# Down projection of a SwiGLU layer: a ninth weight tile in seven products, and two held plain tiles instead of three

## The chip, the cores and the metric

The kernel runs on one core of one Trainium2 chip. The metric is the device time of one execution in microseconds (us). A core has a matmul engine (TensorE, PE in the profile), a vector engine (VectorE, DVE), a scalar engine (ScalarE, ACT), a general engine (GpSimd, POOL) and a queue engine (SyncE, SP) that issues most of the transfers. Each engine works through its own instructions in order; semaphores make one wait for another.

## The reference

One decoder block on 256 tokens of width 1024, in float32: two token mixers side by side, an output projection, a layer norm, a SwiGLU feed-forward layer, and a second layer norm. The change lies in the last step, the down projection of the feed-forward layer.

```python
D_MODEL = 1024
SEQ = 256
D_FF = ((8 * D_MODEL + 3 * 256 - 1) // (3 * 256)) * 256   # 2816
...
    mixed = jnp.einsum('bsc,cd->bsd', g_a * z_a + g_b * z_b, w_out)
    x = layer_norm(DN_ALPHA * x + mixed, ln1_w, ln1_b)

    h = jnp.einsum('bsd,df->bsf', x, w_ffn_in)
    h_gate, h_up = jnp.split(h, 2, axis=-1)
    y = jnp.einsum('bsf,fd->bsd', jax.nn.silu(h_gate) * h_up, w_ffn_down)
    return layer_norm(DN_ALPHA * x + y, ln2_w, ln2_b)
```

## The kernel before

**Weights.** All weights are cut into 77 tiles of 128 x 2048 numbers (`plan`), each loaded once into one of three `raw` buffers by SP. A float32 product is made from three faster ones: ACT casts the tile to a short form (`wh`), DVE subtracts that from the original (`wl`), and PE adds up `wh` times the high part of the activations, `wl` times the high part, and `wh` times the low part. `stage` and `stage_fast` do this for the next tile of the list, and `fetch` calls them so that three items stand ready ahead of the one handed out. There are four `wh` and four `wl` buffers. In the last stage the order of PE, DVE and ACT is the order of the program; the other queues are ordered by the compiler's scheduler, which also hands out the buffers of each pool, among them 12 slots of 128 x 2048 (`big`, through `slot`).

**The down projection.** It has 11 tiles, each for 256 rows of `w_ffn_down` (a pair of 128) and all 1024 columns. A tile times its activations is a product of 2 x 2 blocks: two halves of the tokens by two blocks of rows by two halves of the columns, eight block products of 512 columns, three matmuls each, so 24 matmuls. A *fast* tile (`fast`, from line 1050) does it with seven block products of sums of blocks, 21 matmuls, as in Strassen's scheme. It needs seven blocks of activation sums (made in `ffn_step`, lines 1026 to 1031: four operations of DVE and one split) and seven blocks of weights: three of the four quarters of the tile as they are (`corners`) and four sums of quarters (`sums`). The item `corners` is used by 9 matmuls, then `sums` by 12.

The string `DOWN` gives the order: `S` is a fast tile whose weight sums DVE makes in SBUF (three additions, `make_sums`), `T` a fast tile whose sums are made by transfers in DRAM and then loaded, `P` a plain tile. Before, it is `STTSTTSTPPP`: eight fast tiles (the column pairs `FAST`, 2 to 9), then three plain ones (`PLAIN`, the pairs 0, 1 and 10). `sum_weights` makes one T tile's sums: two copies on SP's queue and four accumulating transfers on POOL's, each of the last two after what it reads. It is called behind the loads of the tiles in `SUMS_AFTER`. `BESIDE` lists the raw items that are loaded into a slot of `big` instead of a `raw` buffer.

Token half 0 and half 1 share the banks `p1`, `p5`, `p6` and `p7` in the fast tiles; `into_residual` (line 1061) adds these to the residual on DVE after the last fast tile.

**The held tiles.** The last `HOLD_DOWN` tiles are plain and held. In the loop they are multiplied for token half 0 alone (12 matmuls each), so that half 0's layer norm can run while PE does half 1. For half 1 PE then does `p3` with the first held tile, two opening matmuls (lines 1139 and 1140), `p3` with the other held tiles, the edge (258 columns, line 1145) and `more` (256 columns, line 1146), 6 matmuls a tile each. The edge's columns hold the sums of the weights' rows too, so the mean of half 1 is known before `more` is done: line 1167 takes it, 1168 to 1171 are the squares on ACT, 1177 and 1178 the variance and its root, 1181 the output. ACT's copies into the edge and `more` banks (lines 1141 to 1143) come behind the opening matmuls and ahead of half 0's squares (line 1154). The squares of half 0 are needed by line 1158.

**The activations' pairs.** Pairs 0 and 1 are computed early (`FfnEarly`). Pair 10 comes out of the last `ffn_step`; before, it is a plain tile's, its product is handed back as `last_gate` and split after the first fast tile (line 1081). The activation sums of each fast pair live in a slot, but for the first (spare tiles) and the last (the unused half of a plain slot, and the tile `masks`).

Of the kernel before, what the change touches and what calls it, by code (L numbers as in the profile page):

```python
# [10 lines left out]
F32 = mybir.dt.float32  # L11
F32R = mybir.dt.float32r
U32 = mybir.dt.uint32
# [4 lines left out]
P = 128  # L18
# [6 lines left out]
NF = FF // P  # L25
LEVELS = 7
# [10 lines left out]
BLOCKS = 32  # L37
GROUPS = ((0, 1), (2, 3), (4, 5, 6))
HQ_WIDE = 4
HOLD_DOWN = 3  # L40
SUMS = 2
ORDERED = 2
LAGS = (0,1,3,5)
DOWN = "STTSTTSTPPP"
SUMS_AFTER = (36, 41, 50, 54, 58)
FAST = tuple(range(2, 2 + len(DOWN) - DOWN.count("P")))
PLAIN = tuple(q for q in range(NF // 2) if q not in FAST)
SEQUENCE = [PLAIN[DOWN[:i].count("P")] if s == "P" else FAST[i - DOWN[:i].count("P")] for i, s in enumerate(DOWN)]
BESIDE = ((3, "corners"), (4, "sums"), (6, "corners"), (7, "corners"), (7, "sums"))
SUMMED = [q for q, s in zip(SEQUENCE, DOWN) if s == "T"]  # L50

C_ID = 0
# [3 lines left out]
C_MASK = C_CAUSAL + 3 * P  # L56
C_END = C_MASK + LEVELS * P
# [27 lines left out]
def plan():  # L85

    tiles = []

    def add(w, k0, kn, c0, n, held=False):
        tiles.append((w, k0, kn, c0 if isinstance(c0, tuple) else (c0,), n, held))  # L90

    def feat(w, c0, n):
        for c in range(c0, c0 + n, 256):
            add(w, 0, 8, c, 256)

    def tok(w, c0, n):
        for c in range(c0, c0 + n, 512):
            add(w, 0, 4, c, 512)
            add(w, 4, 4, c, 512)

    feat("w_in", 0, 1024)
    tok("w_in", 2048, 1024)
    tok("w_in", 3072, 1024)
    tok("w_in", 6144, 512)
    tok("w_in", 8192, 1024)
    for c in range(2):
        if c == 1:
            tok("w_in", 6144 + 512, 512)
        for j in range(2 * c, 2 * c + 2):
            feat("w_in", 5120 + j * 256, 256)  # L110
            feat("w_in", 4096 + j * 256, 256)
    tok("w_in", 7168, 1024)
    tok("w_branch_a", 0, 1024)
    tok("w_branch_b", 0, 1024)
    for k in range(0, KC, 2):
        add("w_out", k, 2, 0, 1024)
    for j in range(0, EARLY, 2):
        for k in range(0, KC, 4):
            add("w_ffn_in", k, 4, (j * P, FF + j * P), 256, j < HOLD_IN)
    for j in range(EARLY, NF, 2):  # L120
        add("w_ffn_in", 0, 8, j * P, 256)
        add("w_ffn_in", 0, 8, FF + j * P, 256)
    for q in SEQUENCE:
        add("w_ffn_down", 2 * q, 2, 0, 1024)
    return tiles
# [3 lines left out]
def hybrid_layer_kernel(ctx: ExitStack, tc, x, xw, vecs, bias, wts, ln1_w, ln1_b, ln2_w, ln2_b, consts, out):  # L129
    nc = tc.nc  # L130
    pool = lambda name, bufs, **kw: ctx.enter_context(tc.tile_pool(name=name, bufs=bufs, **kw))
    cp = pool("cp", 1)
# [12 lines left out]
    def r32(ap):  # L145
        return ap.bitcast(F32)
# [31 lines left out]
    tiles = plan()  # L178
# [4 lines left out]
    ready = []  # L183
    held_down = range(len(tiles) - HOLD_DOWN, len(tiles))
    last_raw = []
    corners = {}
# [4 lines left out]
    def split(dst_h, dst_l, src):  # L191
        nc.scalar.copy(dst_h, src)
        nc.vector.tensor_sub(dst_l, src, r32(dst_h))
# [5 lines left out]
    def stage(pieces=None, eng=nc.vector):  # L199
# [18 lines left out]
        for ks in ks_of(pieces or (k,)):  # L218
            nc.sync.dma_start(raw[:, ks, :], src[:, ks, :])
            if i in SUMS_AFTER and ks.start == 0:  # L220
                sum_weights(down[SUMMED[SUMS_AFTER.index(i)]])
            nc.scalar.copy(h[:, ks, :], raw[:, ks, :])  # L222
# [7 lines left out]
    def sum_weights(i):  # L230


        b, s = quarters(wts[i]), quarters(summed[i])
        tc.keep_in_program_order(nc.sync.dma_start(s[:, 0:2, :], b[:, 1:3, :]))
        tc.keep_in_program_order(nc.sync.dma_start(s[:, 2:4, :], b[:, 2:4, :]))
        more = lambda dst, src: nc.gpsimd.dma_start(dst, src, accum_op=ALU.add)  # L236
        for n in range(2):
            more(s[:, n, :], b[:, 0, :])
        more(s[:, 2, :], s[:, 0, :])
        more(s[:, 3, :], s[:, 2, :])  # L240

    def stage_fast(i, kind):


        def make_sums(b):
# [7 lines left out]
        at = SEQUENCE.index(next(q for q in FAST if down[q] == i))  # L253
        raw = lambda: quarters(slot(f"raw{kind}{i}") if (at, kind) in BESIDE else
                               wraw.tile([P, 2048], F32, tag="raw", name=f"raw{kind}{i}"))
# [47 lines left out]
    xp = Pair("xp")  # L303
    xTh, xTl = Pair.Part(xp, 0), Pair.Part(xp, 1)
    vec = cp.tile([P, 3 * H], F32, tag="vec", name="vec")
    cst = cp.tile([P, C_MASK], F32, tag="cst", name="cst")
    msk = cp.tile([P, C_END - C_MASK], F32, tag="masks", name="masks")
    ident = cst[:, C_ID:C_ID + P]
    causal = cst[:, C_CAUSAL:C_MASK]
    cos = cst[:, C_COS:C_COS + T]  # L310
    sin = cst[:, C_SIN:C_SIN + T]
    masks = msk.bitcast(U32).rearrange("p (l t) -> p l t", l=LEVELS)
    ones = cp.tile([P, P], F32R, tag="ones", name="ones")
    half = cp.tile([P, 4], F32, tag="half", name="half")

# [110 lines left out]
    with tc.manual_schedule(engines={ET.PE, ET.DVE, ET.Activation}):  # L426
# [40 lines left out]
        add(range(4, 8))  # L467
        for f in range(4, 8):
            forget(f)
    for z, a, b in ((cst, 0, C_MASK), (msk, C_MASK, C_END)):  # L470
        tc.keep_in_program_order(nc.sync.dma_start(z, consts[:, a:b]))
    for j in range(4):
        sg = sm.tile([P, 2, T], F32, tag="sg", name=f"sgq{j}")
        sgs = [by_half(sg[:, f, :]) for f in range(2)]
        if j < HQ_WIDE:
            for f, ps in enumerate(wide_pair(f"hq{j}", xp, mm, "mm")):
                z = Qg[:, :, 2 * j + f, :]
# [413 lines left out]
    def row_parts(name, widths, n0=0):  # L891
        parts = []
        for i, (p, w) in enumerate(widths):
# [9 lines left out]
    apl = [slot(f"ap{i}", F32R).rearrange("p (q u k t) -> p q u k t", q=2, u=2, k=2)  # L903
           for i in range((len(PLAIN) + 1) // 2)]
    act_plain = {q: apl[i // 2][:, i % 2] for i, q in enumerate(PLAIN)}

    def fast_parts(i):
        if i == 0:
            tiles = [klp.tile([P, H * P], F32R, tag="kl", name="ash"), cp.tile([P, D], F32R, tag="bgr", name="asl")]
        elif i == len(FAST) - 1:  # L910
            tiles = [apl[-1][:, 1].rearrange("p u k t -> p (u k t)"), cp.tile([P, 7 * P], F32R, tag="masks", name="asl7")]
        else:
            both = slot(f"as{i}", F32R)
            tiles = [both[:, 0:1024], both[:, 1024:2048]]
        return [z[:, 0:7 * P].rearrange("p (b t) -> p b t", b=7) for z in tiles]
# [46 lines left out]
    with tc.manual_schedule(engines={ET.PE, ET.DVE, ET.Activation}):  # L962
# [3 lines left out]
        tiles = [(2 * q,) + fetch(0) for q in range(4)]  # L966
# [42 lines left out]
    room = slot("room").rearrange("p (n b t) -> p n b t", n=2, b=8)  # L1009
    def ffn_step(j):  # L1010
        q = j // 2
        z = room[:, q % 2]
        gate, up = [z[:, b:b + 4, :].rearrange("p (f t) c -> p f (t c)", f=2) for b in (0, 4)]
        for nm, p, tag, s in [("g", mm, "mm", gate), ("u", aux, "aux", up)]:
            for f, ps in enumerate(wide_pair(f"f{nm}{j}", x1p, p, tag)):
                nc.scalar.copy(s[:, f, :], ps[:, 1, :])
                nc.vector.tensor_add(s[:, f, :], ps[:, 0, :], s[:, f, :])
            if nm == "g":
                nc.scalar.activation(s, s, AF.Silu)
        nc.vector.tensor_mul(gate, gate, up)  # L1020
        if q in PLAIN:
            if q < NF // 2 - 1:
                split(act_plain[q][:, 0], act_plain[q][:, 1], gate)
            return gate

        nc.vector.tensor_sub(z[:, 4, :], z[:, 0, :], z[:, 2, :])
        nc.vector.tensor_sub(z[:, 5, :], z[:, 4, :], z[:, 1, :])
        nc.vector.tensor_sub(z[:, 6, :], z[:, 1, :], z[:, 0, :])
        nc.vector.tensor_add(z[:, 7, :], z[:, 3, :], z[:, 5, :])
        act_fast[q] = fast_parts(FAST.index(q))  # L1030
        split(*act_fast[q], z[:, 1:8, :])
# [3 lines left out]

    with tc.manual_schedule(engines={ET.PE, ET.DVE, ET.Activation}):
        for j in range(NF - 2 * ORDERED, NF, 2):
            last_gate = ffn_step(j)
        bank = lambda p, n: p.tile([P, 512], F32, tag="aux" if p is aux else "mm", name=n)
        p2, p4, p1, p5 = [bank(mm, f"wp{i}") for i in (2, 4, 1, 5)]  # L1040
        p7, p3, wd0, p6 = [bank(aux, f"wp{i}") for i in (7, 3, 0, 6)]
# [35 lines left out]
        for i, q in enumerate(SEQUENCE):  # L1077
            if q in FAST:
                fast(q)
                if q == FAST[0]:  # L1080
                    split(act_plain[PLAIN[-1]][:, 0], act_plain[PLAIN[-1]][:, 1], last_gate)
                if q == FAST[-1]:
                    wb2 = bcast("wb2", ln2_w, ln2_b)
                    into_residual()
                continue
            tile_q = [(2 * q,) + fetch()]
            if i < len(SEQUENCE) - HOLD_DOWN:
                for part in late:
                    rows_pass([part], lhs, 1, tile_q, first=2 * begins[id(part[0])], **ends)
            else:  # L1090
                held += tile_q
            for part in early:
                rows_pass([part], lhs, 0, tile_q, first=2 * begins[id(part[0])], **ends)
        y = slot("y").rearrange("p (t d) -> p t d", t=NT)
        z, spare = [slot("z")[:, i:i + D] for i in (0, D)]
# [3 lines left out]

        ends_h, ends_l = [slot(f"e{n}", F32R)[:, 0:HOLD_DOWN * 2 * 264].rearrange("p (i k c) -> p i k c", i=HOLD_DOWN, k=2)  # L1100
                          for n in "hl"]
        edges = []
        sums = sm.tile([P, 2 * HOLD_DOWN], F32, tag="bst", name="wsum")
        for i, (raw, (k0, wh, wl)) in enumerate(zip(last_raw, held)):
# [112 lines left out]
```

## Time and profile before

| | |
|---|---|
| median of 3 runs | 485.95 us (485.85 to 488.02) |
| the profiled execution | 485.77 us |
| its span, first to last instruction | 484.0 us |
| PE busy | 476.5 us, 2956 matmuls |
| DVE busy | 387.8 us |
| ACT busy | 294.1 us |
| POOL busy | 58.2 us |
| DMA | 108.70 MB, mean 225 GB/s |
| the fast tiles | 422.57 to 460.77 us |
| the held tiles | 460.77 to 477.73 us |
| the rest, without PE | 477.73 to 484.0 us |

The profile is of one execution. Its span begins with the first instruction and ends with the last; the device time is 1.8 us more. Matmuls overlap, so PE's busy time tells that it had work, not how fast it was; the distance between the starts of two matmuls tells that.

### The profile page before, as it was taken

To read this page: it belongs to the slowest core of one execution; us is meant where nothing else is said; L and a number is where in the kernel's file an instruction comes from. 1 tells how busy PE (TensorE), PEld (TensorE's weight loads), DVE (VectorE), ACT (ScalarE), POOL (GpSimd) and SP (SyncE) were. 2 spreads that over 40 slices of the span, in tenths; PEclk is the share of its full clock that TensorE was granted. 3 is DMA by queue.
4 is the path that set the end of the run, shared out by engine and by line. 5 is a ranking of instruction groups with operands and counts; after the bars stand their busy time and mean duration, and the time that the engine had idled before them with its cause. 6 is when DMAs were issued, how large, how long until landed. Compare 5 with 4: busy or idle time off the path is not lost.

```text
span 484.0 us, 7438 instructions
## 1 busy us (share of the span) xinstructions
PE 476.5 (98%) x2956; PEld 409.0 (85%) x2956; DVE 387.8 (80%) x504; ACT 294.1 (61%) x408; POOL 58.2 (12%) x62
## 2 busy tenths in 40 slices
PE   9999999999999999999999999999999999999994
PEld 8888888788899888888888888888888888888884
DVE  4889895799957889999566778853887778799995
ACT  6698666447575687864743353444566655576852
POOL 0000000000024522420201000022020000000130
PEclk9999999999999999999999999999999999999999
DMA  8987437622753255558979855499999744599442
GB/s 309 416 310 265 175 114 291 215 107 101 274 202 136 96 193 192 173 182 290 288 225 297 244 190 197 153 285 280 302 296 269 240 175 153 156 396 420 179 110 87
DMA packets 21811, 108.70 MB, mean 225 GB/s; under 512 B 2448, under 2 KB 4240, under 8 KB 12176
## 3 DMA queue, kind: packets, MB, share of 16 engines
q1 hardware_dynamic: 16272, 98.13, 55.3%
q0 software_dynamic: 5360, 9.96, 10.3%
q8 instruction: 23, 0.38, 0.3%
q10 hardware_dynamic: 144, 0.13, 0.1%
q14 instruction: 12, 0.10, 0.1%
HBM read 105.59 MB, written 11.53 MB: 242 GB/s over the span
## 4 chain that ended last, share of the span: by engine, by line
PE 96%; issue 1%; DMA 1%; ACT 1%; DVE 0%; DVEq 0%; POOLq 0%; POOL 0%; SPq 0%
PE fu L351 7%; PE fg L351 7%; PE fg L353 3%; PE fu L353 3%; PE hq L351 3%; PE wp L1059 3%; PE wp L1058 3%; PE wp L1057 3%; PE mq L351 2%; PE mk L351 2%; PE gb L402 2%; PE mv L402 2%; PE hg L402 2%; PE hq L353 2%; PE hf L376 2%; PE mv L404 2%
## 5 line engine op out<-in xcount | busy, mean ns | idle before, releaser
L224 DVE TENSOR_TENSOR wl<-raw,wh 128x2048 fp32r<-128x2048 f32 (+1 forms) x70 | 160.2, 2294 | 53.8 <-ACT wh L222 53.5
L222 ACT CAST wh<-raw 128x2048 fp32r<-128x2048 f32 (+1 forms) x70 | 131.6, 1888 | 56.8 <-PE fg L351 14.0
L351 PE MATMUL fg<-x1p,wh 128*128 128x512 f32 x144 | 50.5, 394 | 0.0
L351 PE MATMUL fu<-x1p,wh 128*128 128x512 f32 x144 | 50.4, 394 | 0.0
L353 PE MATMUL fg<-x1p,wl 128*128 128x256 f32 x144 | 40.0, 278 | 0.0
L353 PE MATMUL fu<-x1p,wl 128*128 128x256 f32 x144 | 39.9, 277 | 0.0
L351 PEld LDWEIGHTS fu<-x1p,wh 128*128 128x128 f32 x144 | 27.0, 187 | 6.2
L351 PEld LDWEIGHTS fg<-x1p,wh 128*128 128x128 f32 x144 | 27.0, 187 | 6.1
L353 PEld LDWEIGHTS fg<-x1p,wl 128*128 128x128 f32 x144 | 27.1, 188 | 0.1
L353 PEld LDWEIGHTS fu<-x1p,wl 128*128 128x128 f32 x144 | 27.1, 188 | 0.0
L754 POOL TENSOR_TENSOR rtk<-rtk,cst 128x512 f32<-128x512 f32 x4 | 6.2, 1561 | 163.4 <-ACT rtk L752 163.4
L351 PE MATMUL hq<-xp,wh 128*128 128x512 f32 x64 | 22.2, 394 | 0.0
L353 PE MATMUL hq<-xp,wl 128*128 128x256 f32 x64 | 17.7, 277 | 0.0
L351 PE MATMUL mq<-xp,wh 128*128 128x512 f32 x48 | 17.0, 398 | 0.0
L351 PE MATMUL mk<-xp,wh 128*128 128x512 f32 x48 | 16.7, 395 | 0.0
L236 POOL DMA_DIRECT2D sums<-sums x10 | 8.1, 812 | 65.1 <-DMA sums<-in_wts_dram 33.0
L269 DVE TENSOR_TENSOR wlcorners<-rawcorners,whcorners 128x1536 fp32r<-128x1536 f32 x8 | 14.0, 1752 | 2.1 <-ACT whcorners L266 2.1
L351 PEld LDWEIGHTS hq<-xp,wh 128*128 128x128 f32 x64 | 12.0, 188 | 2.8
L236 POOL DMA_DIRECT2D sums<-in_wts_dram x10 | 8.4, 989 | 42.2 <-DMA sums<-in_wts_dram 42.2
L353 PE MATMUL mq<-xp,wl 128*128 128x256 f32 x48 | 13.2, 281 | 0.0
L353 PE MATMUL mk<-xp,wl 128*128 128x256 f32 x48 | 12.8, 277 | 0.0
L402 PE MATMUL mv<-wh,xp 128*128 128x512 f32 x32 | 12.7, 398 | 0.0
(373 smaller groups left out, 1337.5 us busy)
## 6 DMA issues: line engine op xcount, KB each, us to landing
raw<-in_wts_dram SPq DMA_DIRECT2D x68, 1024.0 KB, 5.3
sums<-in_wts_dram SPq DMA_DIRECT2D x10, 512.0 KB, 8.6
rawsums<-sums SPq DMA_DIRECT2D x4, 1024.0 KB, 8.3
xw<-in_xw_dram SPq DMA_DIRECT2D x6, 640.0 KB, 9.0
rawcorners<-in_wts_dram SPq DMA_DIRECT2D x5, 768.0 KB, 5.7
rawcorners<-in_wts_dram SPq DMA_DIRECT2D x3, 1024.0 KB, 6.2
sums<-in_wts_dram POOLq DMA_DIRECT2D x10, 256.0 KB, 9.1
sums<-sums POOLq DMA_DIRECT2D x10, 256.0 KB, 6.5
```

The source lines that it names most:

```text
L222: nc.scalar.copy(h[:, ks, :], raw[:, ks, :])
L224: eng.tensor_sub(l[:, ks, :], raw[:, ks, :], r32(h[:, ks, :]))
L236: more = lambda dst, src: nc.gpsimd.dma_start(dst, src, accum_op=ALU.add)
L269: nc.vector.tensor_sub(l, b[:, 1:4, :], r32(h))
L351: nc.tensor.matmul(ps, wh[:, k, wcol], a.both(k), start=(k == 0), stop=False)
L353: nc.tensor.matmul(ps[:, 0, :], wl[:, k, wcol], a[0, k, slice(0, T)], start=False, stop=(k == KC - 1))
L376: nc.tensor.matmul(ps, wh[:, kk, wcol], xp.both(k), start=False, stop=False)
L402: nc.tensor.matmul(pss[t], ah[:, kk, ts], wh[:, k, :], start=(kk == 0), stop=False)
L404: nc.tensor.matmul(pss[t], ah[:, kk, ts], wl[:, k, :], start=False, stop=(kk == KC - 1))
L1057: nc.tensor.matmul(ps, ah[:, a, :], wh[:, b, :], start=(q == begins[id(ps)]), stop=False)
L1058: nc.tensor.matmul(ps, ah[:, a, :], wl[:, b, :], start=False, stop=False)
L1059: nc.tensor.matmul(ps, al[:, a, :], wh[:, b, :], start=False, stop=stop)
```

## The change

A ninth tile becomes fast, and seven of the nine get their sums from DRAM. The order is `STTTTTSTTPP`: `FAST` is 2 to 10, `PLAIN` 0 and 1, and two tiles are held. Two more sums are made, behind tiles 32, 35, 38 and 41 where it was 36 and 41. The last pair, 10, is now a fast pair. Its gate product stays in `room`, and its activation sums and split (`fast_act`) come after the fourth fast tile. Their tile is a slot of `big`, as for the other pairs; the constants and the masks are one tile and one load instead of two.

```diff
-HOLD_DOWN = 3
+HOLD_DOWN = 2
...
-DOWN = "STTSTTSTPPP"
-SUMS_AFTER = (36, 41, 50, 54, 58)
+DOWN = "STTTTTSTTPP"
+SUMS_AFTER = (32, 35, 38, 41, 50, 54, 58)
...
-BESIDE = ((3, "corners"), (4, "sums"), (6, "corners"), (7, "corners"), (7, "sums"))
+BESIDE = ((3, "corners"), (5, "corners"), (6, "corners"), (7, "corners"), (7, "sums"), (8, "corners"))
...
-    cst = cp.tile([P, C_MASK], F32, tag="cst", name="cst")
-    msk = cp.tile([P, C_END - C_MASK], F32, tag="masks", name="masks")
+    cst = cp.tile([P, C_END], F32, tag="cst", name="cst")
...
-    for z, a, b in ((cst, 0, C_MASK), (msk, C_MASK, C_END)):
-        tc.keep_in_program_order(nc.sync.dma_start(z, consts[:, a:b]))
+    tc.keep_in_program_order(nc.sync.dma_start(cst, consts))
...
-        elif i == len(FAST) - 1:
-            tiles = [apl[-1][:, 1].rearrange("p u k t -> p (u k t)"), cp.tile([P, 7 * P], F32R, tag="masks", name="asl7")]
         else:
             both = slot(f"as{i}", F32R)
...
         if q in PLAIN:
-            if q < NF // 2 - 1:
-                split(act_plain[q][:, 0], act_plain[q][:, 1], gate)
-            return gate
-
+            split(act_plain[q][:, 0], act_plain[q][:, 1], gate)
+            return
+        if q < FAST[-1]:
+            fast_act(q)
+
+    def fast_act(q):
+        z = room[:, q % 2]
         nc.vector.tensor_sub(z[:, 4, :], z[:, 0, :], z[:, 2, :])
         nc.vector.tensor_sub(z[:, 5, :], z[:, 4, :], z[:, 1, :])
         nc.vector.tensor_sub(z[:, 6, :], z[:, 1, :], z[:, 0, :])
...
-            last_gate = ffn_step(j)
+            ffn_step(j)
...
                 fast(q)
-                if q == FAST[0]:
-                    split(act_plain[PLAIN[-1]][:, 0], act_plain[PLAIN[-1]][:, 1], last_gate)
+                if q == FAST[3]:
+                    fast_act(FAST[-1])
                 if q == FAST[-1]:
                     wb2 = bcast("wb2", ln2_w, ln2_b)
                     into_residual()
```

More of the change, by code (lines that the diff above doesn't have):

```diff
@@ L311, in hybrid_layer_kernel @@
     sin = cst[:, C_SIN:C_SIN + T]
-    masks = msk.bitcast(U32).rearrange("p (l t) -> p l t", l=LEVELS)
+    masks = cst[:, C_MASK:C_END].bitcast(U32).rearrange("p (l t) -> p l t", l=LEVELS)
     ones = cp.tile([P, P], F32R, tag="ones", name="ones")
```

## The prediction

> **What bounds the kernel now.** I read the busy table first, then who waited for whom on TensorE (PE), then the busy times of three late stretches, then PE's, DVE's (VectorE) and ACT's (ScalarE) timelines from 405 us to the end.
>
> ```profile
> span 484.0 us, 7438 instructions
> PE 476.5 (98%) x2956; PEld 409.0 (85%) x2956; DVE 387.8 (80%) x504; ACT 294.1 (61%) x408; POOL 58.2 (12%) x62
> PE warm L445 <- PEq L1204: 0.8, 1, 0.8
> PE hf L373 <- ACT fh L192: 0.3, 1, 0.3
> 422.57:460.77 38.20, 38.20 (x171) 31.56 (x169) 38.03 (x29) 29.68 (x23) 3.64 (x6) 1.00 0.84 327
> ```
>
> PE waits twice, 1.1 us in all, near the start, and never again. So each microsecond taken from PE's matmuls counts as long as nothing new makes PE wait. The last row is the stretch of the eight fast tiles (its columns: length, then busy time of PE, weight loads, DVE, ACT, POOL, then clock, DMA share, GB/s): DVE is busy 38.03 of 38.20 us. PE is first there by a hair; DVE has no slack to lend.
>
> **The PE sum.** Matmuls overlap, so I price one by the distance between starts, not by its listed 0.39 us.
>
> ```profile
> 422.57 0.39 PE L1057 MATMUL wp<-whcorners,ash 128*128 128x512 f32 x1
> 460.77 0.39 PE L868 MATMUL wp<-wh,ap 128*128 128x512 f32 x1
> 470.29 0.29 PE L1139 MATMUL wp<-wh,ones 128*128 128x258 f32 x1
> 473.28 0.28 PE L868 MATMUL wp<-eh,ap 128*128 128x258 f32 x1
> 475.42 0.29 PE L868 MATMUL more<-wh,ap 128*128 128x256 f32 x1
> 477.45 0.28 PE L870 MATMUL more<-wh,ap 128*128 128x256 f32 x1
> ```
>
> Eight fast tiles of 21 matmuls: 460.77 - 422.57 = 38.20 us, 0.2274 each, 4.775 a tile (its corners, 9 matmuls, take 2.05). From 460.77 to 470.29 stand 42 matmuls (36 of token half 0, 6 of p3): 0.2267 each. A held tile has 18 of these (4.08), 6 at the edge (2.14 / 18 each, 0.71) and 6 of `more` (0.119 each, 0.72): 5.51 us. The change turns one held tile into a fast one: PE loses 5.51 - 4.775 = 0.74 us. That is all the change can earn on PE.
>
> **The tail.** Which chain ends last once PE is done with the fast tiles?
>
> ```profile
> 470.62 0.38 ACT L1141 COPY wp<-y 128x256 f32<-128x256 f32 x1 [5.21 <-PE wp L1139]
> 473.22 0.21 DVE L1158 TENSOR_SCALAR n2sum<-n2sum 128x1 f32<-128x1 f32 x1 [1.02 <-ACT z L1122]
> 474.29 0.75 DVE L1125 SCALAR_TENSOR_TENSOR z<-z,n2sum,wb 128x512 f32<-128x512 f32 x1
> 475.62 0.22 DVE L1167 TENSOR_SCALAR n2sum<-wp,n2sum 128x1 f32<-128x1 f32 x1 [0.58 <-PE wp L870]
> 477.77 0.47 ACT L1122 ACTIVATE z<-more,n2sum 128x256 f32<-128x256 f32 x1 [0.39 <-PE more L870]
> 478.37 0.16 DVE L1177 TENSOR_TENSOR n2sum<-n2sum 128x1 f32<-128x1 f32 x1 [0.39 <-ACT z L1122]
> ```
>
> ACT may copy into the edge bank only when the opening matmul (470.29) is done. Behind that copy, in ACT's order, stand the squares of half 0; DVE's L1158 waits for them, and L1161 to L1163 come before L1167 in DVE's order. This chain is free at 474.29 + 0.75 = 475.04, 4.75 us after the opening matmul; L1167 then waited 0.58 more for PE's edge. From L1167 to L1177 it took 2.75 us, of which 0.39 was the wait for `more`: 2.36 without it. Now PE sets both ends. With two held tiles PE has 6 matmuls of p3, 12 of the edge and 12 of `more` behind the opening pair: the edge is done some 1.36 + 1.43 + 0.25 + 0.3 = 3.3 us after the opening, so the chain's 4.75 sets L1167. With E the end of the fast tiles, the opening comes at E + 30 x 0.2267 = E + 6.80 (before: E + 9.52), and L1177 at E + 6.80 + 4.75 + 2.36 = E + 13.91. Before it was E + 17.60. E moves by 4.775, so without any new wait L1177, and the end with it, comes 4.775 - 3.69 = **1.09 us later**: the shorter cover costs more than the 0.74 earned.
>
> **The order on DVE.** An S tile makes its weight sums on DVE; a T tile loads them. Prices:
>
> ```profile
> 441.83 1.92 ACT L280 CAST whsums<-rawsums 128x2048 fp32r<-128x2048 f32 x1 [1.23 <-PE wp L1059]
> 442.14 1.75 DVE L269 TENSOR_TENSOR wlcorners<-rawcorners,whcorners 128x1536 fp32r<-128x1536 f32 x1
> 443.81 2.28 DVE L283 TENSOR_TENSOR wlsums<-rawsums,whsums 128x2048 fp32r<-128x2048 f32 x1
> 446.01 1.22 DVE L248 TENSOR_TENSOR sumscst<-rawcorners 128x1024 f32<-128x1024 f32 x1
> 450.26 1.22 DVE L289 TENSOR_TENSOR wlsums<-sumscst,whsums 128x1024 fp32r<-128x1024 f32 x1
> 452.54 1.75 DVE L269 TENSOR_TENSOR wlcorners<-rawcorners,whcorners 128x1536 fp32r<-128x1536 f32 x1
> 413.79 0.29 DVE L1026 TENSOR_TENSOR room<-room 128x128 f32<-128x128 f32 x1
> 415.82 1.09 DVE L193 TENSOR_TENSOR asl<-room,ap 128x896 fp32r<-128x896 f32 x1 [1.01 <-ACT ap L192]
> 416.83 1.22 DVE L289 TENSOR_TENSOR wlsums<-sumscst,whsums 128x1024 fp32r<-128x1024 f32 x1
> ```
>
> By starts: T corners 1.67, T sums 2.20, together 3.87 for a tile that PE works 4.775 on; S corners with the sums 4.25, S sums 2.28. The activation sums and split of the pair before the last took 416.83 - 413.79 = 3.04, 1.01 of it waiting for ACT's copy (0.94 there). The first row shows ACT waiting for PE: there are four `wh` buffers, so an item is converted only when the item four earlier (same kind, two tiles before) is used up.
>
> On average the new order is easier: five T tiles in a row, on each of which DVE gains 0.9 us. But the buffers cap what may be kept from that. Fast tile i starts at 422.57 + 4.775 i: t3 436.90, t5 446.45, t6 451.22. Sums 4 start on ACT at t3, are cast by 438.82 and split by 441.02; corners 5 by 442.69. There the new `fast_act` of the last column pair stands: 3.04, to 445.73, and ACT's copy for it ends at 444.69. Only then ACT casts sums 5 (446.6), DVE splits them (448.8); PE needs the low part at t5 + 2.05 + 0.23 = 448.73: 0.1 late. Tile 6 is the S tile: 448.8 + 4.25 = 453.05 against t6 + 0.23 + 0.1 = 451.55: **1.5 late**, 1.6 with the last split's end rather than the next start. Its sums at 455.33 against about 455.2: 0.15. After it come T tiles again: 457.0 against 458.1, 460.9 against 462.9; nothing more. New stall: about 1.85 us (bounds: 0, and 4.6 by the slot rival below; I take what the rows give). DVE is then done with the last split at 467.5, E is 465.55 + 1.85 = 467.4, and the row below gives the rest: `into_residual` takes 468.26 - 463.01 = 5.25, to 472.75, ahead of the opening at 474.2.
>
> ```profile
> 463.01 0.68 DVE L1064 SCALAR_TENSOR_TENSOR x<-x,wp 128x512 f32<-128x512 f32 x1
> 468.26 0.41 DVE L1116 SCALAR_TENSOR_TENSOR y<-x,wp 128x256 f32<-128x256 f32 x1
> ```
>
> **What I take as free.** Two more sums (tiles 32 and 35 instead of 36, and 38) add two SP pairs, eight POOL adds and their traffic at 193 to 260 us.
>
> ```profile
> 209.94 1.46 POOL L754 TENSOR_TENSOR rtq<-rtq,cst 128x512 f32<-128x512 f32 x1 [4.57 <-ACT rtq L752]
> 212.81 0.50 ACT L192 CAST qh<-qT 128x128 fp32r<-128x128 f32 x2
> 220.19 0.39 PE L764 MATMUL s<-kT,qT 128*128 128x128 f32 x2
> 238.28 0.81 POOL L236 DMA_DIRECT2D sums<-sums  x1 [6.34 <-DMA sums<-in_wts_dram]
> 243.70 0.81 POOL L236 DMA_DIRECT2D sums<-sums  x1 [4.61 <-DMA sums<-sums]
> 252.91 1.91 ACT L222 CAST wh<-raw 128x2048 fp32r<-128x2048 f32 x1 [3.57 <-PE za L403]
> ```
>
> At 252.91 ACT waits for PE to free buffers, so slower loads there are hidden. POOL is the weak spot: its adds wait in turn for the DMA before them (6.34 and 4.61 us here), and queued ahead of the last rope product (209.94) they would hold ACT's `qh` cast (212.81, right behind it) and a head's scores on PE (220.19). That head has 220.19 - 212.81 = 7.4 us to spare, so the cost lies between 0 (one wait) and 10.95 - 7.4 = 3.6 us (both). I take 0: two sums are made in that stage already and PE never waits. One load of the constants instead of two moves the same bytes and one SP issue fewer, for a first reader at 89 us: 0. Gains below nothing: none, PE has no wait left to remove.
>
> **Sum.** Span 484.0 + 1.09 + 1.85 = 486.9; the profiled execution took 485.77, so **488.7 us**, against the median of 485.95 (0.18 above that execution). Half a percent of it, 2.4 us, is about what a measurement can tell from no change; 2.75 lies just outside.
>
> **Rivals.**
>
> *DVE keeps up (16%).* If the lump before tile 6 is covered, for instance as `fast_act` slips into a gap, only the tail is left: 485.77 + 1.09 = 486.9, not slower by the bound. For it: T tiles give DVE 0.9 us each. Against: the four buffers.
>
> *The PE sum alone (6%).* Tail still set by PE: 485.77 - 0.74 = 485.0. It needs 1.4 us more between opening and edge than the counts give.
>
> *The new split waits for a slot (18%).* The last pair's `as` tile now takes a slot of the 12-slot pool instead of a spare buffer.
>
> ```profile
> SPq L256 <- PE wp L1059: 6.5, 2, 4.2
> POOL wb L854 <- DVE wlcorners L269: 59.0, 1, 59.0
> ```
>
> Loads already wait for slots that PE frees, and `wb` takes one early. If a later load takes the slot freed at 442.7, `as` gets that of tile 4, at t5 = 446.45: ACT copies to 447.4, DVE splits to 448.5, sums 5 to 451.5, 2.8 late, then the S tile as above: 486.86 + 4.6 = 491.5. It decides when fewer than seven slots are free by 443.7.
>
> *Loads too slow (7%).* T tiles load 0.75 + 1 MiB, 1.835 MB, per 4.775 us.
>
> ```profile
> GB/s 309 416 310 265 175 114 291 215 107 101 274 202 136 96 193 192 173 182 290 288 225 297 244 190 197 153 285 280 302 296 269 240 175 153 156 396 420 179 110 87
> 422.57:455.90 33.33, 33.33 (x149) 27.59 (x148) 33.16 (x27) 25.19 (x19) 1.43 (x3) 1.00 0.89 359
> rawsums<-sums SPq DMA_DIRECT2D x4, 1024.0 KB, 8.3
> ```
>
> At the 359 GB/s of that stretch a T tile takes 5.11 us, 0.34 more than PE; five of them give 1.7 us, 490.4. At the best slice's 420 it takes 4.37 and nothing waits; I follow the best slice, since the stretch's mean holds thin moments. A single load has room too: sums 5 can be asked for when DVE has split sums 3 (436.2); with the median 8.3 they land at 444.5, and ACT casts them at 444.7. The Trainium skill, "DMA: Bandwidth & Descriptors", section Bandwidth, speaks against the change here: HBM binds a load at about 358 GB/s per core (it also lists 425 for a large load with the neighbour core idle). By the 358 a T tile takes 5.13 us, an estimate, and this rival comes about. This trace shows 420 in one slice, so it does not hold throughout here.
>
> *Adds hold the rope on POOL (5%).* Both waits ahead of the last rope product: 3.6 us more, 492.3.
>
> **How the numbers follow.** Forecast 46%; the remaining 2% is for a gain that I can't name. The forecast's own spread (the stall is 1.5 to 2.2) puts a third of it inside the half percent. Slower: 31 + 18 + 6 + 4 = 59%; same 39%; faster 2%. The range 485.9 to 491.6 takes in DVE keeping up, the slot and the loads, and half the way down to the PE sum alone; it leaves out some 10%.
>
> **What would show it.** PE's first wait after the start, 1 to 2 us, at the seventh fast tile's corners, released by DVE L269; ACT's cast of sums 5 right behind the last `as` copy; L1167 no longer waiting for PE but right behind L1163; PE's `more` done over 1 us before ACT squares it. Wrong if PE never waits (then 486.9), if it waits for `as` (491), or if L1167 still waits for PE.

## The result, and the profile after

| | before | after |
|---|---|---|
| median | 485.95 us (5 runs) | 492.11 us (5 runs, 491.14 to 492.52) |
| ratio | | 1.0113, 95% interval 1.0087 to 1.0140 |
| the profiled execution, its span | 485.77, 484.0 us | 492.22, 490.4 us |
| first matmul of the feed-forward layer (`fg`) | 322.25 us | 325.83 us |
| the fast tiles | 422.57 to 460.77 us | 426.15 to 471.35 us |
| variance of half 1 on DVE (L1177, now L1176) | 478.37 us | 485.14 us |

The change is slower: by 1.1% in the ratio, and by 6.2 us in the medians, where after lies half a microsecond above the top of the predicted range (491.6). The ratios here are of means; that of this table leaves out one slow run of before, 530.03 us, and keeps one of 488.02, so it is smaller than the ratio of the medians. Line numbers of after are one to four lower than in before, from line 308 on. The head of the page of after:

```profile
span 490.4 us, 7437 instructions
PE 478.1 (97%) x2947; PEld 408.4 (83%) x2947; DVE 386.6 (79%) x505; ACT 293.8 (60%) x403; POOL 64.8 (13%) x67
```

PE's waits in after, without the two at its start (waiting instruction, what released it, us in total, times, longest):

```profile
PE pt L781 <- DVE ms L776: 1.5, 2, 1.3
PE wp L1057 <- DVE wlcorners L269: 1.2, 1, 1.2
PE s L762 <- ACT p L786: 0.6, 1, 0.6
PE wp L1057 <- DVE wlsums L283: 0.3, 1, 0.3
```

Before, PE waited for nothing after its start. Now it has two groups of waits: two lines in the score stage (`s`, `pt`), which no line of the diff names, and two in the fast tiles. PE's timeline of after says when each group is paid:

```profile
325.83 0.39 PE L350 MATMUL fg<-x1p,wh 128*128 128x512 f32 x1
426.15 0.39 PE L1056 MATMUL wp<-whcorners,ash 128*128 128x512 f32 x1
455.29 0.39 PE L1056 MATMUL wp<-whcorners,as 128*128 128x512 f32 x1
456.91 0.50 PE L1057 MATMUL wp<-wlcorners,as 128*128 128x512 f32 x1 [1.24 <-DVE wlcorners L269]
471.35 0.39 PE L866 MATMUL wp<-wh,ap 128*128 128x512 f32 x1
```

The variance comes 485.14 - 478.37 = 6.77 us later than before, in three parts:

- **3.58 us** are there when `fg` starts (325.83 - 322.25; 0.15 of it from the start of the run: PE's first matmul of `hq` comes at 27.80 instead of 27.64), 100 us before the down projection.
- **2.2 us** are a stall in the fast tiles: they took 45.20 us, and 38.20 + 4.775 = 42.98 would be nine at the pace of before. By the starts of their matmuls seven took 4.76 to 4.79 each, the sixth 5.31 and the seventh, the S tile, 6.55 (the mean of before, 4.775, has a last tile of 4.85 in it). The third and fourth row show the gap at the S tile: 1.62 us where 0.23 is usual.
- **1.0 us** is the tail: from the end of the fast tiles to the variance it took 13.79 us, 3.81 less than the 17.60 of before, where the ninth fast tile adds 4.775.

Behind the variance both kernels do the same; the span of after grew by 6.4 only because what follows the landing of the last store took 1.0 us instead of 1.3.

**The score stage.** POOL's two last rope products are that for k (`rtk`) and that for q (`rtq`). In before q's began at 209.94 us, and k's stood as follows in POOL's and ACT's timelines:

```profile
202.66 1.33 POOL L754 TENSOR_TENSOR rtk<-rtk,cst 128x512 f32<-128x512 f32 x1 [4.91 <-ACT rtk L752]
204.07 1.29 POOL L755 TENSOR_TENSOR kT<-kT,rtk 128x512 f32<-128x512 f32 x1
205.41 0.44 ACT L192 CAST keys<-kT 128x256 fp32r<-128x256 f32 x1
```

POOL's timeline of after:

```profile
207.74 0.81 POOL L236 DMA_DIRECT2D sums<-sums  x1 [4.46 <-DMA sums<-in_wts_dram]
208.29 1.58 POOL L752 TENSOR_TENSOR rtk<-rtk,cst 128x512 f32<-128x512 f32 x1
214.10 0.84 POOL L236 DMA_DIRECT2D sums<-sums  x1 [2.86 <-DMA sums<-sums]
214.66 1.59 POOL L752 TENSOR_TENSOR rtq<-rtq,cst 128x512 f32<-128x512 f32 x1
```

ACT's waits of after between 150 and 300 us:

```profile
ACT keys L192 <- POOL kT L753: 5.6, 1, 5.6
ACT qh L192 <- POOL qT L753: 3.4, 1, 3.4
```

The last two additions of the new sum behind tile 32 stand in POOL's order right ahead of the last two rope products. Each waits for the transfer before it, and POOL waits with it: the product for k starts at 208.29, 5.6 us late, and that for q at 214.66, 4.7 us late. ACT's casts of the keys and of q pay next. In before the cast of the keys followed the k product within 0.05 us, so it had no time to spare. What PE then loses is more than its listed waits say (1.5 + 0.6), since some distances between matmuls grow without a listed wait; the shift of `fg` is the number to use.

**The fast tiles.** DVE's timeline of after:

```profile
446.48 0.28 DVE L1025 TENSOR_TENSOR room<-room 128x128 f32<-128x128 f32 x1
448.50 1.09 DVE L193 TENSOR_TENSOR as<-room,as 128x896 fp32r<-128x896 f32 x1 [1.01 <-ACT as L192]
450.31 2.29 DVE L283 TENSOR_TENSOR wlsums<-rawsums,whsums 128x2048 fp32r<-128x2048 f32 x1 [0.72 <-ACT whsums L280]
452.52 1.22 DVE L248 TENSOR_TENSOR sumscst<-rawcorners 128x1024 f32<-128x1024 f32 x1
455.11 1.75 DVE L269 TENSOR_TENSOR wlcorners<-rawcorners,whcorners 128x1536 fp32r<-128x1536 f32 x1
```

This is the predicted order. The last pair's sums and split take from 446.48 to 449.59, the sums split that they held up begins at 450.31, the S tile's own additions at 452.52, and its corners are split at 456.86, when PE has waited for them since 455.5.

**The tail.** DVE's timeline of after:

```profile
481.09 0.21 DVE L1157 TENSOR_SCALAR n2sum<-n2sum 128x1 f32<-128x1 f32 x1 [0.90 <-ACT z L1121]
482.02 0.75 DVE L1124 SCALAR_TENSOR_TENSOR z<-z,n2sum,wb 128x512 f32<-128x512 f32 x1
482.69 0.21 DVE L1166 TENSOR_SCALAR n2sum<-wp,n2sum 128x1 f32<-128x1 f32 x1
485.14 0.16 DVE L1176 TENSOR_TENSOR n2sum<-n2sum 128x1 f32<-128x1 f32 x1
```

Before, the mean of half 1 waited 0.58 us for PE and the variance 0.39 us for `more`. Both waits are gone: L1166 follows half 0's output on DVE at once. PE is done early and the chain of ACT and DVE sets the end.

### The profile page after: what moved, and what is told of

It is laid out like the page before. It is cut to its first block, busy times and chain, and to the rows that moved or that the text cites. A ratio compares the mean times of both kernels' runs of the same rounds, so it can differ in the third digit from the quotient of the medians.

```text
span 490.4 us, 7437 instructions
## 1 busy us (share of the span) xinstructions
PE 478.1 (97%) x2947; PEld 408.4 (83%) x2947; DVE 386.6 (79%) x505; ACT 293.8 (60%) x403; POOL 64.8 (13%) x67
## 4 chain that ended last, share of the span: by engine, by line
PE 79%; DVE 6%; ACT 5%; DMA 4%; issue 3%; POOL 2%; DVEq 0%; POOLq 0%; SPq 0%; ACTq 0%
PE fu L350 7%; PE fg L350 7%; PE fg L352 3%; PE fu L352 3%; PE hq L350 3%; DVE wl L224 2%; PE wp L1057 2%; PE wp L1058 2%; PE wp L1056 2%; DMA rawcorners<-in_wts_dram 2%; DMA sums<-in_wts_dram 2%; PE mv L401 2%; PE hg L401 2%; PE gb L401 2%; PE hq L352 2%
## 5 line engine op out<-in xcount | busy, mean ns | idle before, releaser
L224 DVE TENSOR_TENSOR wl<-raw,wh 128x2048 fp32r<-128x2048 f32 (+1 forms) x69 | 157.5, 2288 | 56.2 <-ACT wh L222 55.9
L222 ACT CAST wh<-raw 128x2048 fp32r<-128x2048 f32 (+1 forms) x69 | 129.7, 1886 | 57.4 <-PE fg L350 14.0
L236 POOL DMA_DIRECT2D sums<-sums x14 | 11.5, 818 | 92.4 <-DMA sums<-in_wts_dram 47.7
L269 DVE TENSOR_TENSOR wlcorners<-rawcorners,whcorners 128x1536 fp32r<-128x1536 f32 x9 | 15.8, 1751 | 2.1 <-ACT whcorners L266 2.1
L236 POOL DMA_DIRECT2D sums<-in_wts_dram x14 | 12.1, 1009 | 30.9 <-DMA sums<-in_wts_dram 30.7
L283 DVE TENSOR_TENSOR wlsums<-rawsums,whsums 128x2048 fp32r<-128x2048 f32 x6 | 13.7, 2290 | 2.9 <-ACT whsums L280 2.9
L266 ACT CAST whcorners<-rawcorners 128x1536 fp32r<-128x1536 f32 x9 | 13.3, 1477 | 0.8 <-DMA rawcorners<-in_wts_dram 0.7
L280 ACT CAST whsums<-rawsums 128x2048 fp32r<-128x2048 f32 x6 | 11.5, 1913 | 3.7 <-PE wp L1058 3.7
```

What stands on the lines that cost most here:

```text
L224: eng.tensor_sub(l[:, ks, :], raw[:, ks, :], r32(h[:, ks, :]))
L266: nc.scalar.copy(h, b[:, 1:4, :])
L269: nc.vector.tensor_sub(l, b[:, 1:4, :], r32(h))
L280: nc.scalar.copy(h[:, bs, :], z)
L283: nc.vector.tensor_sub(l[:, bs, :], z, r32(h[:, bs, :]))
```

## The experiments

The theory: three separate costs. The sum of tile 32 blocks POOL (3.5), DVE's lump meets the S tile (2.2), and the tail's cover is too short (1.0). Against the first stood that the extra DRAM traffic of the sums, not POOL's order, slows the stage; against the others, that the loads or a late slot make PE wait.

**sums_late**: every sum is made one place later, none behind tile 32.

```diff
-SUMS_AFTER = (32, 35, 38, 41, 50, 54, 58)
+SUMS_AFTER = (35, 38, 41, 50, 54, 58, 62)
```

> The changed kernel with its seven sums made behind tiles 35, 38, 41, 50, 54, 58 and 62, so none is made before the last rope product on POOL; nothing else differs. Theory (POOL's queue: the adds of the first sum stand ahead of the last two rope products): PE's two waits at 212 and 241 us are gone, the feed-forward layer starts at 322.2 us as in the kernel before instead of 325.8, span 490.4 - 3.5 = 486.9, time about 488.6. Rival (traffic: more sums made on the DMA engines at 193 to 290 us slow what the attention needs): three sums stand there instead of four and two, so at least half of the 3.5 stays, span 488.6 or more.

Measured 488.40 us, ratio 1.0053 (1.0038 to 1.0068), span 486.6. `fg` starts at 322.01, the waits for `s` and `pt` are gone, and those in the fast tiles are what they were. PE's waits, without the two at its start:

```profile
PE wp L1057 <- DVE wlcorners L269: 1.2, 1, 1.2
PE wp L1057 <- DVE wlsums L283: 0.3, 1, 0.3
```

So one number of the change, 32, was worth 3.7 us of its 6.2 by the medians; counted from PE's first `hq`, which comes 0.35 us earlier here than in after, it is 3.5. The seven sums are still made, so it is not their count.

**rope_on_dve**: the sum stays behind tile 32, and the last pair of rope products goes to DVE.

```diff
-        nc.gpsimd.tensor_mul(tmp, tmp, bc(sin))
-        nc.gpsimd.tensor_add(dst[:, hs, :], dst[:, hs, :], tmp)
+        eng = nc.vector if j == 3 else nc.gpsimd
+        eng.tensor_mul(tmp, tmp, bc(sin))
+        eng.tensor_add(dst[:, hs, :], dst[:, hs, :], tmp)
```

> The changed kernel with the rope products of the last pair of heads (both of k and of q) on DVE instead of POOL; the sums stay where they are. Theory (POOL's queue): nobody waits for POOL any more, the 3.5 us go, less up to 1 us for some 2.7 us of extra DVE work: span 487 to 488. Rival (traffic): the transfers are the same, so PE waits as before, span 490.4 or more.

Measured 488.37 us, ratio 1.0050 (1.0035 to 1.0065), span 486.4; no wait of PE in the score stage. The span is 0.6 us below the expected range, so the extra work of DVE cost nothing that shows. The same transfers run at the same place (POOL issues them from 200.64, at 207.41 and at 213.69 us, in after from 201.13, at 207.74 and at 214.10) and cost nothing once nothing stands behind them on POOL. That rules out the traffic.

**before_sum32**: the kernel before, with its first sum moved from tile 36 to 32.

```diff
-SUMS_AFTER = (36, 41, 50, 54, 58)
+SUMS_AFTER = (32, 41, 50, 54, 58)
```

> The kernel before with one sum moved: its first sum behind tile 32 instead of 36; everything else, the eight fast tiles and three held ones too, is the kernel before. Theory (POOL's queue): this alone costs 3.5 us, span 487.5, time 489.4. Rival (traffic): the same bytes, five sums in all, so no more than some tenths, span 484 to 484.6.

Measured 489.32 us, ratio 1.0067 (1.0050 to 1.0084). PE's waits in this kernel:

```profile
PE pt L783 <- DVE ms L778: 1.4, 1, 1.4
PE s L764 <- ACT p L788: 1.1, 1, 1.1
```

And its POOL timeline:

```profile
214.47 0.83 POOL L236 DMA_DIRECT2D sums<-sums  x1 [2.55 <-DMA sums<-sums]
215.04 1.58 POOL L754 TENSOR_TENSOR rtq<-rtq,cst 128x512 f32<-128x512 f32 x1
```

The same picture as in after, in a kernel that has nothing else of the change: one sum at this place costs 3.3 us by the medians.

**lump_early**: the last pair's sums and split come one tile earlier.

```diff
-                if q == FAST[3]:
+                if q == FAST[2]:
                     fast_act(FAST[-1])
```

> The changed kernel with the last pair's activation sums after the third fast tile instead of the fourth. Theory (the lump of 3.04 us and the S tile's 4.25 us fall on DVE one behind the other, with only four buffers of lead): DVE wins back 0.9 us ahead of the S tile, PE's wait at its corners falls from about 1.5 to about 0.7, span 489.5. Rival A (the S tile alone makes PE wait, wherever the lump stands): span 490.4. Rival B (the lump alone): the whole 1.8 us go, span 488.6.

Measured 491.01 us, ratio 1.0103 (1.0088 to 1.0118). PE's waits in the fast tiles:

```profile
PE wp L1057 <- DVE wlcorners L269: 0.4, 1, 0.4
PE wp L1057 <- DVE wlsums L283: 0.3, 1, 0.3
```

The S tile took 5.64 us instead of 6.55, a gain of 0.9 at the place the theory names; the wait for the sums of a T tile moved one tile ahead with the lump. So the lump's place, and with it DVE's order, makes one half of the S tile's stall. The other half, 0.9, stays, with the S tile's own additions behind the lump as before. That it is no slot is read from the trace: ACT's copy began as soon as DVE's sums were done (below).

**tail** and **before_tail**: the same reordering of DVE's last instructions, in after and in before. Half 1's sum over `p3` goes ahead of half 0's variance, and half 1's mean ahead of half 0's outputs. The cut shows the first place; in the second, the centring of the edge goes behind half 1's variance.

```diff
-        nc.vector.tensor_scalar(col(st, 6), col(st, 4), col(st, 5), LN_EPS, op0=ALU.add, op1=ALU.add)
-        nc.gpsimd.tensor_tensor(col(st, 7), col(st, 6), half[:, 0:1], op=ALU.pow)
...
-        scaled(z, z, halves[0], col(st, 7), 0)
+        nc.vector.tensor_scalar(col(st, 6), col(st, 4), col(st, 5), LN_EPS, op0=ALU.add, op1=ALU.add)
+        nc.gpsimd.tensor_tensor(col(st, 7), col(st, 6), half[:, 0:1], op=ALU.pow)
...
...
+        scaled(z, z, halves[0], col(st, 7), 0)
...
```

> The changed kernel with DVE's last instructions in another order: half 1's sum over p3 and its mean (taken from the edge) ahead of half 0's outputs, and half 0's second output ahead of half 1's variance. Theory (the chain from the opening matmul over ACT's copies, half 0's squares and half 0's outputs sets the end): the mean no longer stands behind half 0's output, it follows PE's edge within 0.2 us, the variance stands 5.7 us behind the opening instead of 6.86; span 490.4 - 1.1 = 489.3, between 489.0 and 489.7. Rival (PE's `more` sets the end, as before): span 490.4.

> The kernel before with the same new order of DVE's last instructions. Theory: with three held tiles PE's edge and `more` set the end, so nothing is won: span 483.8 to 484.2. Rival (the old order costs time of itself, whatever the cover): a gain of some 1 us here too, span 483.

In after: 490.90 us, ratio 1.0104 (1.0089 to 1.0120), span 489.2, 1.2 less. From the end of the fast tiles to the variance it is 12.76 us instead of 13.79, so 1.0 is the edit's and the rest lies ahead of it. In before: 485.76 against 485.68, ratio 1.0002 (0.9993 to 1.0011). The same edit wins 1.0 us where DVE's chain sets the end and nothing where PE does. This is the change of bound that the prediction gave for the tail.

**late_lump_tail**: the edits of sums_late, lump_early and tail together.

> The changed kernel with three edits together: no sum before the last rope product (sums behind tiles 35, 38, 41, 50, 54, 58, 62), the activation sums after the third fast tile, the new order of DVE's last instructions. If the three costs add up: 490.4 - 3.6 - 0.9 - 1.1 = 484.8, time 486.6, 0.9 us of PE's waits at the S tile being left.

Measured 486.81 us, ratio 1.0022 (1.0013 to 1.0032), span 484.5. The spans can't simply be added, since the executions start up to 0.5 us earlier than that of after. From PE's first `hq`, sums_late brings the variance 3.5 us forward; the fast tiles are 0.9 shorter in lump_early, and the tail is 1.0 shorter in tail. That makes 5.4, and late_lump_tail brings the variance 5.35 forward (5.3 by the medians). The costs add up, as separate ones do.

**all_fixed**: no S tile but the first, so that DVE has no additions to make behind the lump, which stays; eight sums, and the tail's order.

```diff
-DOWN = "STTTTTSTTPP"
-SUMS_AFTER = (32, 35, 38, 41, 50, 54, 58)
+DOWN = "STTTTTTTTPP"
+SUMS_AFTER = (35, 38, 41, 50, 53, 56, 59, 62)
...
```

> The changed kernel with the late sums and the new last order, and with the S tile at place 6 made a T tile (eight sums from DRAM, behind tiles 35, 38, 41, 50, 53, 56, 59, 62). Theory (the S tile's additions behind the lump make PE wait): PE's waits in the fast tiles fall from 1.8 to 0.1, span 490.4 - 3.6 - 1.7 - 1.1 = 484.0, at best 483.7; time 485.5 to 485.8, the kernel before within the measurement. Rival (loads too slow for T tiles in a row): PE or ACT waits for DMA in the fast tiles, span over 485.

Measured 487.49 us, ratio 1.0037 (1.0024 to 1.0049), span 486.1: a miss by 2.1 us. The stall did go: PE's only wait in the fast tiles is 0.3, and they end at 465.89. But look who ACT waits for between 420 and 475 us:

```profile
ACT whsums L280 <- DMA rawsums<-sums: 2.1, 1, 2.1
ACT whcorners L266 <- DMA rawcorners<-in_wts_dram: 1.2, 1, 1.2
ACT wh L222 <- DMA raw<-in_wts_dram: 1.1, 2, 0.6
```

DVE's timeline of all_fixed, its last split of weight sums and the start of `into_residual`:

```profile
460.45 2.29 DVE L283 TENSOR_TENSOR wlsums<-rawsums,whsums 128x2048 fp32r<-128x2048 f32 x1 [2.15 <-ACT whsums L280]
467.60 0.68 DVE L1063 SCALAR_TENSOR_TENSOR x<-x,wp 128x512 f32<-128x512 f32 x1
```

And the stretch of the late loads (length, busy time of PE, weight loads, DVE, ACT, POOL, clock, DMA share, GB/s):

```profile
442.00:460.00 18.00, 17.74 (x78) 14.33 (x77) 14.54 (x12) 12.22 (x8) 1.15 (x2) 1.00 1.01 412
```

The DMA engines are full, at 412 GB/s. A T tile loads 1.75 MiB where the S tile loads 1, and the last sums were asked for at 443.70 and landed at 458.41. So DVE's last split is late, and with it `into_residual`: 467.60, 1.7 us after PE had done the fast tiles. The tail begins with that. The rival of slow loads is real; in after it does not show, since ACT waits only 0.7 us there for a load.

**best**: late_lump_tail, and the last pair's four activation sums made by POOL after the first fast tile, so that the lump on DVE is the split alone.

```diff
...
+                if q == FAST[0]:
+                    fast_sums(FAST[-1], nc.gpsimd)
-                if q == FAST[3]:
+                if q == FAST[2]:
                     fast_act(FAST[-1])
```

> After with all that the earlier runs point to: the seven sums behind tiles 35, 38, 41, 50, 54, 58 and 62, the tail's order, the last pair's split after the third fast tile, and that pair's four activation sums on GpSimd after the first fast tile instead of on VectorE. Theory (three separate costs; what is left of the stall at the S tile is VectorE's lump): PE's waits in the fast tiles fall from 0.6 (late_lump_tail) to 0.3 or less, span 483.9 to 484.3 against 484.5 there, time 485.9 to 486.2: level with the kernel before, since PE's 0.74 saved is given back by the shorter cover of the tail. Rival (POOL's queue is as tight in the down projection as in the score stage): the four sums stand behind a transfer that POOL issues, the split comes late, PE waits 1 us or more in the fast tiles and the time is 487 or above.

Measured 485.62 us against 485.89, ratio 1.0003 (0.9990 to 1.0015). Its twelve executions lie in two groups, eight from 484.97 to 485.67 and four from 487.12 to 488.00, and the profiled one is of the second (span 485.6). The time is level with before, as expected; the trace is not as expected. PE's wait in the fast tiles:

```profile
PE wp L1062 <- DVE wlcorners L269: 0.7, 1, 0.7
```

ACT's longest wait for a load between 420 and 480 us:

```profile
ACT whsums L280 <- DMA rawsums<-sums: 4.1, 2, 3.1
```

And the stretch behind it, columns as above:

```profile
442.00:458.00 16.00, 15.28 (x66) 12.06 (x66) 13.37 (x10) 10.17 (x7) 1.17 (x2) 1.00 1.01 410
```

Of the two waits of late_lump_tail (0.3 each) that for the sums is gone and that for the S tile's corners has grown, and in this execution it comes from a load: ACT waits 3.1 us for weight sums, and DVE idles 2.56 us for ACT before it splits them, ahead of the S tile's additions and corners. The stretch behind it moves 410 GB/s at full share. POOL's four sums cost nothing on the path, though POOL took 5.71 us for three of them that DVE does in 0.3 each.

**best_wb**: best, with the last layer norm's weight and bias loaded by SP behind the last weight tile instead of by POOL at 443.5 us.

```diff
+        if name == "wb2":
+            tc.keep_in_program_order(nc.sync.dma_start(t[:, 0, :], w[0].partition_broadcast(P)))
+            tc.keep_in_program_order(nc.sync.dma_start(t[:, 1, :], b[0].partition_broadcast(P)))
+            return t
```

> The kernel best with one edit: the second layer norm's weight and bias (1 MB, broadcast to 128 partitions) are loaded by SP behind the last weight tile, not by POOL at 443.5 us in the middle of the T tiles' loads. Theory (with VectorE's lump gone, the loads are the next limit: from 442 to 458 the profiled execution of best moved 405 to 416 GB/s at a full DMA share, its last tile landed at 463.1, 15 us after it was asked for, and VectorE's last split ended at 467.4 instead of about 466): the last tile lands some 2.5 us earlier (1 MB at 410 GB/s), VectorE's last split ends by 466.2, and all executions lie where the lower eight of best's twelve lay, 485.0 to 485.7. Rival (the four executions of best at 487.1 to 488.0 come of something else, such as the sums tile's load that ScalarE waited 3.1 us for, asked for 7 us before by a queue that waited for a buffer): ScalarE's wait of 3 us and PE's of 0.7 stay, and so does the second group of times.

Measured 485.75 us against 485.83, ratio 1.0006 (0.9997 to 1.0015). The last tile landed at 457.94 instead of 463.12, and DVE's last split ended at 464.99 instead of 467.46. That is the way the theory says, but the tile came 5.2 us earlier where 2.5 were expected, and the two profiled executions are of different groups, so how much of it is the edit's is not shown. The second group of times did not go: eight executions took 485.50 to 486.13, three 486.50 to 487.25. In the profiled one, of the first group, PE waits for nothing after its start, and the fast tiles' end and PE's last matmul stand in its timeline as shown below. The page of best_wb:

```profile
span 483.7 us, 7439 instructions
```

PE's timeline of best_wb:

```profile
465.31 0.39 PE L870 MATMUL wp<-wh,ap 128*128 128x512 f32 x1
476.50 0.28 PE L872 MATMUL more<-wh,ap 128*128 128x256 f32 x1
```

PE is done 477.45 - 476.50 = 0.95 us earlier than before, 0.12 of it from an earlier start. The variance is only 0.31 earlier (478.06), as DVE's chain sets the end. What the second group of times comes from stays open. The load that ACT waited for in best was asked for at 436.56 and landed at 443.60; in best_wb the same load went from 436.46 to 441.23. The layer norm's load began at 443.53, too late to explain that, so the length of one load differs between executions, and whether that alone makes the second group was not settled.

## Why the prediction was wrong where it was, and right where it was

- **What I take as free** is the step that failed: "I take 0" for the additions on POOL, which measured 3.3 to 3.7 us (before_sum32, sums_late). The prediction named the mechanism, POOL held by its additions, and gave both ends, 0 and 3.6. Its reason for the 0 was that "two sums are made in that stage already and PE never waits". But the first of those stood on POOL at 238 and 244 us, behind the last rope product of before (209.94). The new one's traffic begins at 193 by the prediction's own words, and in after its additions were issued from 201 to 214, around the last two products. Place in the queue decided, and it could have been worked out from the rows that were there. That the measured cost is the upper end is luck, though: 3.6 was two waits of 10.95 us less 7.4 that the product for q could be late. In after that product began 4.7 late and ACT's cast of q 6.8 late, which by this sum costs nothing. The sum left out the product for k, which the first of the two additions held up by 5.6 us and whose cast on ACT had no time to spare. How the loss divides between the two products, no run shows. The rival *adds hold the rope on POOL* was given 5%.
- **The order on DVE** held. Forecast 1.85 us, measured 2.2: 0.55 at the sixth tile (forecast 0.1) and 1.79 at the S tile (1.6 and 0.15), both against 4.76, together 2.34; the 2.2 is against 4.775, the mean of before. The stall at the sums of the sixth tile was mis-sized; DVE began that split 0.1 later than forecast, after the 3.58 are taken off, and there was no slack for it. lump_early shows that half of the S tile's stall hangs on the place of the lump; that at the same place a T tile makes PE wait for nothing (all_fixed) shows that the S tile's additions are needed for it too.
- **The tail** held: forecast 1.09 later, measured 0.97. The opening matmul came at 478.16, 6.81 us after the fast tiles (6.80), the mean's instruction 4.53 after that (4.75), the variance 2.45 later (2.36). tail and before_tail show the change of bound.
- **The PE sum** held: 0.74 forecast, 0.83 in best_wb, the version in which PE waits for nothing. As forecast, it is given back: there the variance is only 0.2 earlier, the start of the run taken off.
- **The slot** did not come about: ACT's copy for the last pair started at 447.53, as DVE's sums ended at 447.49.
- **Loads too slow** was no cost in after, where ACT waited 0.7 us once for a load in that stage, but became one in all_fixed and best, when DVE no longer held the order up. A T tile's 1.835 MB take 4.45 us at 412 GB/s, less than PE's 4.76, so the rate alone would do. I put the cost down to the time between a buffer's release and the landing of its next load; no run tests that by itself. The Trainium skill, "DMA: Bandwidth & Descriptors", section Bandwidth, gives a limit of about 358 GB/s per core for such loads, and 425 for one large load with the neighbour idle. The trace disagrees with the first and stays under the second: all_fixed moved 412 GB/s over 18 us, and before already 417 from 426 to 442 us, where the prediction had gone by one slice.
- **What would show it**: the wait at the seventh tile, the mean right behind half 0's output and PE's early `more` (482.54, squared by ACT at 484.34) all came. "PE's first wait after the start" was wrong: that is in the score stage, and in the fast tiles the sixth tile's 0.3 us comes before the seventh's.

The sum: forecast 1.09 + 1.85 + 0 = 2.94; measured 0.97 + 2.22 + 3.58 = 6.77 at the variance, 6.4 in the span. That the range ends so near the measured time is luck as well: its top, 491.6, stood there for the rival of the slot, which did not come.

## What to carry to other kernels

When a transfer is added to the queue of an engine that also computes, write down which of that engine's own instructions stand behind it and when they are needed; a transfer that must wait for another one holds them all, however idle the engine looks. A last stage that is covered by PE has two chains with one end: before shortening PE's work there, work out how much shorter it may get until the other chain sets the end. And a stall removed at one engine shows the next limit only then, so the fixes of a change are worth trying together.

## What the runs showed of the hardware that was not expected

- An engine that is 13% busy can hold the program: POOL's two waits for transfers (4.46 and 2.86 us) became 9.0 us of waits on ACT and put PE 3.4 us behind, counted from its first `hq`.
- With the DMA share full and other loads asked for before it, a load takes much longer than its size tells: the last plain tile (1 MiB) took 15.2 us from issue to landing in best, against 5.9 us in the median of its kind.
- Executions start some tenths of a microsecond apart: PE's first `hq` comes between 27.27 (late_lump_tail) and 28.00 us (before_tail) in the profiles here, and before_tail, whose code is that of before up to there, is 0.36 later than before. Spans that differ by less are compared from a common matmul.
